# The per-layer embedding gate of a hybrid trunk: tokens as rows, and seven block products in place of eight

## The chip, the cores and the metric

The kernel runs on one core of one Trainium2 chip. The metric is the device time of one execution in microseconds (us). The engines are named as the profile names them: PE is TensorE's matmuls and PEld its weight loads, DVE is VectorE, ACT ScalarE, POOL GpSimd, SP SyncE, which here only issues transfers.

## The reference: what is computed

A trunk of four layers over 512 tokens of width 1024, in f32. Layer i uses a token mixer (gated linear attention GLA, latent attention MLA, a short convolution, and GLA again), then a squared-ReLU MLP of width 4096, then an embedding gate of its own:

```python
x = layer_norm(ALPHA * x + h, ln_g[i, 0], ln_b[i, 0])
x = layer_norm(ALPHA * x + sq_relu_mlp(x, mlp_w1[i], mlp_w2[i]), ln_g[i, 1], ln_b[i, 1])
x = x + jax.nn.sigmoid(x @ ple_w_gate[i]) * (p[i] @ ple_w_proj[i])
```

The change is in the third line: a 512x1024 by 1024x1024 product (the gate), and beside it a 512x256 by 256x1024 product (the projection).

## The kernel before, in words

**Matmuls.** Every f32 operand that matters is split into a high part (a cast to fp32r on ScalarE, line 87) and a low part (the difference, on VectorE, line 88). `mm3` (lines 113 to 117) then makes three matmuls of each product: high by high, high by low, low by high. Weights come by SyncE's queue into one of 4 buffers `raw` of 1 MB (`wget`, line 92) and are split in two pieces of 1024 columns (`wsplit`) into one of 4 buffers `wh`/`wl`. So at most four weights stand ready, and a split can't begin before an older weight has been used up. Activations and other large tiles share ten buffers named `r`, half-width ones eight named `t`; PSUM has eight banks, `ps`.

**Order.** TensorE runs in the order in which the program emits its instructions. For the other engines the framework draws up a fixed order when it builds the program; the kernel does not set it, apart from a few "issue after" edges. Work that TensorE is to do a little later is put into a list, `pend`, and run from it at set places (`flush`).

**MLP.** `up(g)` makes 512 columns of the hidden layer as a transposed activation, `down(g)` multiplies 1024 of them by their block of `mlp_w2` and adds the result into the residual tiles `xn[0..3]`, 128 tokens by 1024 each, tokens as rows. `down` already works by Winograd's form of Strassen's scheme: the 512x1024 by 1024x1024 product is cut into 2x2 blocks, and seven block products (`product`) do instead of eight, at the price of sums of activation blocks (lines 302, 305, 312, 315) and of weight blocks (`wadd`, line 108). Each product is 2 groups of 12 matmuls of 512 columns, and what it leaves in PSUM is added to `xn` on VectorE (lines 287, 289). The last one, `down(3)`, also normalises: `ln_half` takes the statistics of a half tile (line 151), `ln_apply` applies them (lines 155 to 159).

**The gate, `ple`.** It works with features as rows. First the projection, 8 groups of 6 matmuls, copied out by ScalarE (line 336); between these groups `ln_tr` transposes the four normalised tiles (line 165) and splits them, which gives the transposed x in high and low parts. Then 8 groups, one for each 128 output features, of 24 matmuls of 512 columns each (`stat_group`): for each, VectorE sums the two parts of x back (line 351), ScalarE takes the sigmoid (366), VectorE multiplies by the projection and adds x (367, 368). The result, still features as rows, is split for the next layer; and for the residual it is transposed back by TensorE (line 377, `back`, through `pend`), copied by ScalarE (380) and stored to DRAM in eight column blocks (381). In the last layer it goes to the output (370; the last block in two halves, lines 360 to 363), which the host turns.

**The next layer.** GLA starts with the first two heads' keys, MLA with a token-major latent product, the convolution with its `c` block. Each takes the transposed x as it is and flushes the remaining transposes of `pend` early on.

Of the kernel before, what the change touches and what calls it, by code (L numbers as in the profile page):

```python
# [18 lines left out]
P = 128  # L19
# [30 lines left out]
def trunk(ctx: ExitStack, tc: tile.TileContext, I: dict, out: bass.AP, layers=range(DEPTH)):  # L50
# [155 lines left out]

    def add_norm(lhs, unit, xn, gb, scaled, pre=None):
# [23 lines left out]
    def mlp(i, x, xn):  # L231
# [24 lines left out]

        def down(g, gb=None):
            h0, h1 = hid.pop(2 * g), hid.pop(2 * g + 1)  # L260
            lo, hi = slice(0, 256), slice(256, 512)
            a11, a21, a12, a22 = h0[:, :, lo], h0[:, :, hi], h1[:, :, lo], h1[:, :, hi]
            sts = [small(12, f"st{t}", 1) for t in range(NT)] if gb is not None else None
            banks = {}
            fresh = set()

            def weights(hf, c):
                return wget(I["mlp_w2"][i, hf, 2 * g + c])


            def product(a, w, name, th, hf, op):
                st = ring([P, 2, 4, 256], F32R)
                split(st[:, 0], st[:, 1], a)
                wh, wl = v3(wsplit(w), 512)
                for q in range(2):
                    first = (name, q) not in banks
                    if first:
                        banks[name, q] = bank()
                    ps = banks[name, q]
                    c = slice(q * P, q * P + P)  # L280
                    for k in range(4):
                        mm3(ps, (st[:, 0, k, c], st[:, 1, k, c]), (wh[:, k, :], wl[:, k, :]),
                            first and k == 0, k == 3, not first)
                    t = 2 * th + q
                    z = xn[t][:, hf * 512 : hf * 512 + 512]
                    if g == 0 and (t, hf) not in fresh:
                        V.scalar_tensor_tensor(out=z, in0=z, scalar=ALPHA, in1=ps, op0=ALU.mult, op1=op)
                    else:
                        V.tensor_tensor(out=z, in0=z, in1=ps, op=op)  # L289
                    fresh.add((t, hf))  # L290
                    if gb is not None and (th, hf, name) in ((0, 0, "d"), (0, 1, "b"), (1, 0, "c"), (1, 1, "b")):
                        if (t, hf) not in halves:
                            halves.add((t, hf))
                            ln_half(xn[t], sts[t], hf)
                            if (t, 1 - hf) in halves:
                                ln_apply(xn[t], sts[t], gb)

            halves = set()
            add, sub = ALU.add, ALU.subtract
            b11, b12, b22 = weights(0, 0), weights(1, 0), weights(1, 1)  # L300
            product(a11, b11, "b", 0, 0, add)
            V.tensor_tensor(out=a11, in0=a11, in1=a21, op=sub)
            wadd(b22, b12)
            product(a11, b22, "c", 1, 1, sub)
            V.scalar_tensor_tensor(out=a11, in0=a11, scalar=-1.0, in1=a22, op0=ALU.mult, op1=sub)
            wadd(b22, b11)
            product(a11, b22, "b", 1, 0, add)
            b21 = weights(0, 1)
            product(a12, b21, "d", 0, 0, add)
            wadd(b22, b21)  # L310
            product(a22, b22, "c", 1, 0, add)
            V.tensor_tensor(out=a21, in0=a22, in1=a21, op=sub)
            wadd(b12, b11)
            product(a21, b12, "b", 1, 1, sub)
            V.scalar_tensor_tensor(out=a11, in0=a11, scalar=-1.0, in1=a12, op0=ALU.mult, op1=sub)
            product(a11, weights(1, 1), "b", 0, 1, sub)
# [8 lines left out]
        return new_xT()  # L325

    def ple(i, x, xn, last):
        pT = v3(wload(I["pT"][i], 1024), 512)
        wp = v3(wload(I["ple_proj"][i]), 1024)
        proj = [ring([P, 4, T]) for _ in range(2)]  # L330
        for db in range(KB):
            ps = bank()
            for k in range(2):
                c = slice(db * P, db * P + P)
                mm3(ps, (wp[0][:, k, c], wp[1][:, k, c]), (pT[0][:, k, :], pT[1][:, k, :]), k == 0, k == 1)
            A.copy(proj[db // 4][:, db % 4, :], ps)
            if db in (0, 1, 5, 7):
                t = {0: 2, 1: 3, 5: 0, 7: 1}[db]
                ln_tr(t, xn[t], *x)
        if not last:  # L340
            nh, nl = new_xT()
            xd = dp.tile([T, D], F32, tag="xd", name=nm("xd"))
        else:
            nh = nl = xd = None
        ins = None
        for db in range(KB):
            if db % 2 == 0:
                wg = v3(wload(I["ple_gate"][i, db // 2]), 256)
            xh, xl = xk(x, db)
            xs = tmp()  # L350
            V.tensor_tensor(out=xs, in0=f(xh), in1=f(xl), op=ALU.add)
            sg = tmp()
            if last and db == KB - 1:
                ps = bank()
                for q in range(2):
                    sl = slice(256 * q, 256 * q + 256)
                    stat_group(wg, db % 2, x, sl=sl, o=ps)
                for q in range(2):
                    sl = slice(256 * q, 256 * q + 256)
                    A.activation(sg[:, sl], ps[:, sl], AF.Sigmoid)  # L360
                    V.tensor_tensor(out=sg[:, sl], in0=sg[:, sl], in1=proj[db // 4][:, db % 4, sl], op=ALU.mult)  # L361
                    V.tensor_tensor(out=sg[:, sl], in0=sg[:, sl], in1=xs[:, sl], op=ALU.add)  # L362
                    SP.dma_start(out[db * P : db * P + P, sl], sg[:, sl])
                continue
            ps = stat_group(wg, db % 2, x)
            A.activation(sg, ps, AF.Sigmoid)
            V.tensor_tensor(out=sg, in0=sg, in1=proj[db // 4][:, db % 4, :], op=ALU.mult)
            V.tensor_tensor(out=sg, in0=sg, in1=xs, op=ALU.add)
            if last:
                SP.dma_start(out[db * P : db * P + P, :], sg)  # L370
                continue
            ins = split(nh[db // 4][:, db % 4, :], nl[db // 4][:, db % 4, :], sg)

            def back(sg=sg, db=db):
                ps = bank().rearrange("p (t q) -> p t q", q=P)
                for t in range(NT):
                    PE.transpose(ps[:, t, :], sg[:, t * P : t * P + P], ident)
                o = tmp()
                o3 = o.rearrange("p (t q) -> p t q", q=P)
                A.copy(o3, ps)  # L380
                SP.dma_start(xd.rearrange("(t p) d -> p t d", p=P)[:, :, db * P : db * P + P], o3)

            pend.append(back)
            if len(pend) > 2:
                flush(1)
        return (nh, nl), xd, ins
# [11 lines left out]
    def gla(i, j, x, xd, first=None):  # L398
# [9 lines left out]
        for k in range(KB):  # L408
            for h in range(2):
                c = slice(h * P, h * P + P)  # L410
                mm3(pss[h], (w[0][:, k, c], w[1][:, k, c]), xk(x, k), k == 0, k == KB - 1)
# [303 lines left out]
    def mla(i, x, xd, dep):  # L715
# [19 lines left out]
        for t in range(NT):  # L735
            hk = {6: lambda t=t: c_tr(t - 1)} if t else {5: flush}
# [201 lines left out]
    def conv(i, x, xd):  # L938
        oT = []
        xn = None  # L940
        for u in range(4):
# [3 lines left out]
            ct, zt = [], []  # L945
            for cb in range(2):
                ps = stat_group(wc[0], cb, x)
                c = tmp()
                ci = A.copy(c, ps)
                ct.append(c)  # L950
                flush()
# [47 lines left out]
    for i in layers:  # L999
# [6 lines left out]
        x2 = mlp(i, xln, xn)  # L1006
        x, xd, dep = ple(i, x2, xn, i == layers[-1])
# [20 lines left out]
def _layout(a):  # L1028
# [38 lines left out]
    o["ple_gate"] = np.stack([_stat(w) for w in a["ple_w_gate"]])  # L1067
# [23 lines left out]
def build(nc, arrays, layers=range(DEPTH)):  # L1091
# [3 lines left out]
    out = nc.dram_tensor("out_0_dram", (D, T), F32, kind="ExternalOutput").ap()  # L1095
# [13 lines left out]
```

## Time and profile before

| | us |
|---|---|
| median of 3 runs | 2404.61 |
| lowest and highest | 2404.25, 2406.12 |
| the profiled execution's own time | 2405.31 |
| its span, first to last instruction | 2403.4 |
| mean granted TensorE clock | 0.998 |

The span is what the rows of the profile lie in; the time of an execution holds 1.9 us more. In a group's row stand line, engine, operation, output and inputs, shape, count, then busy time and mean length of one, then idle time of the engine ahead of it and what ended it. In a row of the timeline stand start, length, the same names, and in brackets the idle time ahead. In a row of busy times by stage, each engine's busy us and its number of instructions.

### The profile page before, as it was taken

How to read it: one execution, taken by the hardware profiler on the slowest of the kernel's cores; microseconds unless marked ns; L12 is line 12 of the kernel's file. 1: busy time of each engine (PE TensorE's matmuls, PEld its weight loads, DVE VectorE, ACT ScalarE, POOL GpSimd, SP SyncE). 2: the span in 40 equal slices, each digit the busy share in tenths (PEclk: the TensorE clock that was granted, in tenths of full speed). 3: DMA queues.
4: the chain of work that ended last, by engine and by line, in shares of the span. 5: the costliest groups of instructions: out<-in, count | busy, mean ns of one | idle time of the engine just before them, and what ended most of it. 6: DMA issues, size and time to landing. Idle time of an engine off the chain costs nothing. (4 is left out here: it accounts for less than half of the span.)

```text
span 2403.4 us, 28319 instructions
## 1 busy us (share of the span) xinstructions
PE 2375.0 (99%) x11394; PEld 1994.8 (83%) x11394; DVE 1692.8 (70%) x2092; ACT 1077.3 (45%) x1542; POOL 206.7 (9%) x200
## 2 busy tenths in 40 slices
PE   8999999999999999999999999999999999999998
PEld 7888888888888888888888888888887888888887
DVE  7777577689686666688744657768947766766885
ACT  6453445445464354444522244445454443544452
POOL 1541000000000000000000000000005510000000
PEclk9999999999999999999999999999999999999999
DMA  6222242234323222333434224323441222223430
GB/s 230 76 94 99 86 142 89 88 141 150 112 84 110 106 79 97 140 140 114 145 103 156 73 86 140 120 77 129 159 135 53 89 105 106 89 88 139 140 114 35
DMA packets 55346, 267.78 MB, mean 111 GB/s; under 512 B 5680, under 2 KB 18736, under 8 KB 27056
## 3 DMA queue, kind: packets, MB, share of 16 engines
q1 hardware_dynamic: 52272, 256.55, 30.5%
q10 hardware_dynamic: 2304, 8.39, 1.0%
q8 instruction: 89, 1.46, 0.2%
q0 software_dynamic: 640, 1.05, 0.2%
q14 instruction: 41, 0.34, 0.0%
HBM read 256.53 MB, written 8.39 MB: 110 GB/s over the span
## 5 line engine op out<-in xcount | busy, mean ns | idle before, releaser
L88 DVE TENSOR_TENSOR wl<-raw,wh 128x1024 fp32r<-128x1024 f32 x510 | 623.1, 1237 | 356.1 <-ACT wh L87 356.1
L87 ACT CAST wh<-raw 128x1024 fp32r<-128x1024 f32 x510 | 520.1, 1048 | 575.4 <-PE ps L116 262.9
L115 PE MATMUL ps<-r,wh 128*128 128x512 f32 (+1 forms) x1896 | 715.0, 377 | 4.0 <-ACT r L87 4.0
L116 PE MATMUL ps<-r,wh 128*128 128x512 f32 (+1 forms) x1896 | 710.8, 375 | 1.4 <-DVE r L88 0.9
L117 PE MATMUL ps<-r,wl 128*128 128x512 f32 (+1 forms) x1896 | 710.1, 375 | 0.0
L115 PE MATMUL ps<-wh,r 128*128 128x512 f32 x1328 | 520.1, 392 | 0.0
L117 PE MATMUL ps<-wh,r 128*128 128x512 f32 x1328 | 517.0, 389 | 0.0
L116 PE MATMUL ps<-wl,r 128*128 128x512 f32 x1328 | 516.8, 389 | 0.0
L115 PEld LDWEIGHTS ps<-r,wh 128*128 128x128 f32 x1896 | 357.8, 189 | 67.5 <-ACT r L87 5.0
L116 PEld LDWEIGHTS ps<-r,wh 128*128 128x128 f32 x1896 | 357.8, 189 | 66.5 <-DVE r L88 4.1
L117 PEld LDWEIGHTS ps<-r,wl 128*128 128x128 f32 x1896 | 357.5, 189 | 63.7
L117 PEld LDWEIGHTS ps<-wh,r 128*128 128x128 f32 x1328 | 249.3, 188 | 52.0
L115 PEld LDWEIGHTS ps<-wh,r 128*128 128x128 f32 x1328 | 249.4, 188 | 50.7
L116 PEld LDWEIGHTS ps<-wl,r 128*128 128x128 f32 x1328 | 249.5, 188 | 50.6
L147 POOL TENSOR_TENSOR rs<-rs,nhalf 128x1 f32<-128x1 f32 (+2 forms) x44 | 59.8, 1358 | 1826.5 <-DVE rs L146 1826.5
L87 ACT CAST r<-r 128x1024 fp32r<-128x1024 f32 x112 | 116.7, 1049 | 136.2 <-PE ps L117 80.1
L88 DVE TENSOR_TENSOR r<-r,r 128x1024 fp32r<-128x1024 f32 x112 | 136.4, 1221 | 42.4 <-ACT r L87 42.4
L289 DVE TENSOR_TENSOR xn<-xn,ps 128x512 f32<-128x512 f32 x192 | 130.7, 681 | 46.9 <-PE ps L117 46.9
L108 DVE TENSOR_TENSOR raw<-raw,raw 128x1024 f32<-128x1024 f32 x128 | 151.6, 1221 | 1.1
L234 ACT ACTIVATE t<-ps 128x512 f32<-128x512 f32 x128 | 76.1, 595 | 156.0 <-PE ps L117 156.0
L87 ACT CAST r<-ps 128x512 fp32r<-128x512 f32 x84 | 46.6, 591 | 95.1 <-PE ps L165 80.9
L480 ACT ACTIVATE t<-t 128x512 f32<-128x512 f32 (+2 forms) x64 | 37.4, 590 | 107.4 <-POOL t L544 74.9
(192 smaller groups left out, 1865.2 us busy)
## 6 DMA issues: line engine op xcount, KB each, us to landing
raw<-in_mlp_w SPq DMA_DIRECT2D x144, 1024.0 KB, 4.9
raw<-in_ple_gate SPq DMA_DIRECT2D x16, 1024.0 KB, 5.6
raw<-in_conv_in SPq DMA_DIRECT2D x12, 1024.0 KB, 5.0
raw<-in_gla_v SPq DMA_DIRECT2D x8, 1024.0 KB, 5.6
raw<-in_gla_r SPq DMA_DIRECT2D x8, 1024.0 KB, 4.9
raw<-in_gla_out SPq DMA_DIRECT2D x8, 1024.0 KB, 5.0
xd<-t SPq DMA_DIRECT2D x24, 256.0 KB, 3.7
xn<-xd ACTq DMA_DIRECT2D x12, 512.0 KB, 3.9
```

What stands on the lines that cost most here:

```text
L87: A.copy(h, src)
L88: return V.tensor_tensor(out=l, in0=src, in1=f(h), op=ALU.subtract)
L108: V.tensor_tensor(out=dst[:, s], in0=dst[:, s], in1=a[:, s], op=ALU.add)
L115: PE.matmul(o, ah, bh, start=start, stop=False, skip_group_check=more)
L116: PE.matmul(o, ah, bl, start=False, stop=False, skip_group_check=more)
L117: PE.matmul(o, al, bh, start=False, stop=stop, skip_group_check=more)
L147: G.tensor_tensor(out=dst, in0=dst, in1=nhalf[:, :n], op=ALU.pow)
L234: A.activation(r, ps, AF.Relu)
L289: V.tensor_tensor(out=z, in0=z, in1=ps, op=op)
L480: exps.append(A.activation(o, a, AF.Exp, scale=1.0 / TAU))
```

## The change

The seven products of `down` move into a function of their own, `seven(a, b, sink, order, before)`, where `a` and `b` are the four blocks of the activation and of the weight, `order` the order of the products and `sink` what is done with a finished group of 12 matmuls. `down` calls it with its old order, 1, 7, 6, 2, 4, 5, 3.

`ple` is written anew and calls it too. Tokens are now rows of the result. `raw_tr` transposes the normalised tiles without splitting them, `project` makes the projection token by token, and `seven` runs in the order 1, 2, 7, 6, 4, 5, 3, with the blocks so named that products 1 and 2 read tokens 256 to 511. `turn` transposes and splits the finished tiles for the next layer.

```diff
+        def raw_tr(t):
+            for c in range(2):
+                ps = bank().rearrange("p (k q) -> p k q", q=P)
+                for k in range(4):
+                    PE.transpose(ps[:, k, :], xn[t][:, (c * 4 + k) * P : (c * 4 + k + 1) * P], ident)
+                A.copy(xr[c][:, :, t * P : t * P + P], ps)
...
+        def finish(t, hf, src, sign, w):
+            a = acc.pop((t, hf), None) or tmp()
+            for c0 in range(hf * 512, hf * 512 + 512, w):
+                c = slice(c0, c0 + w)
+                b = slice(c0 - hf * 512, c0 - hf * 512 + w)
+                g = a[:, b]
+                A.activation(g, src[:, b], AF.Sigmoid, scale=sign)
+                V.tensor_tensor(out=g, in0=g, in1=proj[t // 2][:, t % 2, c], op=ALU.mult)
+                ins[0] = V.tensor_tensor(out=xn[t][:, c], in0=xn[t][:, c], in1=g, op=ALU.add)
+                if last:
+                    SP.dma_start(out[t * P : t * P + P, c], xn[t][:, c])
+            done.add((t, hf))
+            if not last and (t, 1 - hf) in done:
+                SP.dma_start(xd[t * P : t * P + P, :], xn[t])
+
+        def sink(th, q, hf, ps, op, first, final):
+            t = 2 * (1 - th) + q
+            sign = 1.0 if op == ALU.add else -1.0
+            if first and final:
+                finish(t, hf, ps, sign, 256 if last and q else 512)
+            elif first:
+                acc[t, hf] = tmp()
+                A.mul(acc[t, hf], ps, sign)
+            else:
+                g = acc[t, hf]
+                V.tensor_tensor(out=g, in0=g, in1=ps, op=op)
+                finish(t, hf, g, 1.0, 512)
+            if not last and th == 0 and hf == 1 and q == 0:
+                turn(0)
+
+        def turn(t):
+            if not nx:
+                nx.append(new_xT())
+            ln_tr(t, xn[t], *nx[0])
+
+        raw_tr(2)
+        project(0)
+        raw_tr(3)
+        project(1)
+        project(2)
+        raw_tr(0)
+        project(3)
+        seven((xr[0][:, :, hi], xr[0][:, :, lo], xr[1][:, :, hi], xr[1][:, :, lo]),
+              {f"{c + 1}{hf + 1}": I["ple_gate"][i, hf, c] for c in range(2) for hf in range(2)},
+              sink, (1, 2, 7, 6, 4, 5, 3), {2: [lambda: raw_tr(1)]})
+        if last:
+            return None, None, None
+        turn(1)
+        pend.extend(lambda t=t: turn(t) for t in (2, 3))
+        return nx[0], xd, ins[0]
```

The core of `seven`, in `down` as in `ple`:

```diff
+        plan = {
+            1: (lambda: (a11, get("11")), "b", 0, 0, add),
+            2: (lambda: (a12, get("21")), "d", 0, 0, add),
+            7: (s3, "c", 1, 1, sub),
+            6: (s2, "b", 1, 0, add),
+            4: (t4, "c", 1, 0, add),
+            5: (s1, "b", 1, 1, sub),
+            3: (s4, "b", 0, 1, sub),
+        }
+        for n, p in enumerate(order):
+            ready, name, th, hf, op = plan[p]
+            av, w = ready()
+            st = ring([P, 2, 4, 256], F32R)
+            split(st[:, 0], st[:, 1], av)
+            wh, wl = v3(wsplit(w), 512)
+            for fn in before.get(p, ()):
+                fn()
+            for q in range(2):
...
+                for k in range(4):
+                    mm3(ps, (st[:, 0, k, c], st[:, 1, k, c]), (wh[:, k, :], wl[:, k, :]),
+                        first and k == 0, k == 3, not first)
+                later = any(plan[m][2:4] == (th, hf) for m in order[n + 1 :])
+                sink(th, q, hf, ps, op, (th, hf) not in seen, not later)
```

The functions `s3`, `s2`, `t4`, `s1`, `s4` hold the sums: `s3`, `s2` and `s1` one activation sum and one weight sum each, `t4` a weight sum, `s4` an activation sum and a second fetch of block 22.

Two transposes of the finished tiles (of tiles 2 and 3) remain for the next layer and are run there from `pend`. MLA runs them at steps 2 and 6 of its first group; GLA (of layer 3) and the convolution make their first two groups in halves of 256 tokens, tokens 0 to 255 first, with a flush of one after each. The output is now stored with tokens as rows, and the host no longer turns it; `ple_gate` is laid out in blocks like `mlp_w2`.

More of the change, by code (lines that the diff above doesn't have):

```diff
@@ L203, in nat_group, with seven, get, s3 @@
         return ps
+    def seven(a, b, sink, order, before={}):
+        a11, a21, a12, a22 = a
+        banks, raw, seen = {}, {}, set()
+        add, sub = ALU.add, ALU.subtract
+        def get(n):
+            if n not in raw:
+                raw[n] = wget(b[n])
+            return raw[n]
+        def s3():
+            V.tensor_tensor(out=a11, in0=a11, in1=a21, op=sub)
+            get("12")
+            wadd(get("22"), raw["12"])
+            return a11, raw["22"]
+        def s2():
+            V.scalar_tensor_tensor(out=a11, in0=a11, scalar=-1.0, in1=a22, op0=ALU.mult, op1=sub)
+            wadd(raw["22"], raw["11"])
+            return a11, raw["22"]
+        def t4():
+            wadd(raw["22"], get("21"))
+            return a22, raw["22"]
+        def s1():
+            V.tensor_tensor(out=a21, in0=a22, in1=a21, op=sub)
+            wadd(raw["12"], raw["11"])
+            return a21, raw["12"]
+        def s4():
+            V.scalar_tensor_tensor(out=a11, in0=a11, scalar=-1.0, in1=a12, op0=ALU.mult, op1=sub)
+            return a11, wget(b["22"])
+        plan = {
[16 more added lines that the diff above has]
+            for q in range(2):
+                first = (name, q) not in banks
+                if first:
+                    banks[name, q] = bank()
+                ps = banks[name, q]
+                c = slice(q * P, q * P + P)
+                for k in range(4):
[3 more added lines that the diff above has]
+                sink(th, q, hf, ps, op, (th, hf) not in seen, not later)
+            seen.add((th, hf))
     def add_norm(lhs, unit, xn, gb, scaled, pre=None):
@@ L261, in down @@
             lo, hi = slice(0, 256), slice(256, 512)
-            a11, a21, a12, a22 = h0[:, :, lo], h0[:, :, hi], h1[:, :, lo], h1[:, :, hi]
             sts = [small(12, f"st{t}", 1) for t in range(NT)] if gb is not None else None
[L264 to L296, printed above, removed]
@@ L298, in down @@
-            halves = set()
[L299 to L316, printed above, removed]
+            halves = set()
+            def sink(th, q, hf, ps, op, first, last):
+                t = 2 * th + q
+                z = xn[t][:, hf * 512 : hf * 512 + 512]
+                if g == 0 and first:
+                    V.scalar_tensor_tensor(out=z, in0=z, scalar=ALPHA, in1=ps, op0=ALU.mult, op1=op)
+                else:
+                    V.tensor_tensor(out=z, in0=z, in1=ps, op=op)
+                if gb is not None and last:
+                    ln_half(xn[t], sts[t], hf)
+                    halves.add((t, hf))
+                    if (t, 1 - hf) in halves:
+                        ln_apply(xn[t], sts[t], gb)
@@ L318, in mlp @@
+            seven((h0[:, :, lo], h0[:, :, hi], h1[:, :, lo], h1[:, :, hi]),
+                  {f"{c + 1}{hf + 1}": I["mlp_w2"][i, hf, 2 * g + c] for c in range(2) for hf in range(2)},
+                  sink, (1, 7, 6, 2, 4, 5, 3))
         up(0)
@@ L324, in mlp, with ple @@
         down(3, load_gb(i, 1))
-        return new_xT()
-    def ple(i, x, xn, last):
+    def ple(i, xn, last):
+        lo, hi = slice(0, 256), slice(256, 512)
         pT = v3(wload(I["pT"][i], 1024), 512)
         wp = v3(wload(I["ple_proj"][i]), 1024)
[L330 to L353, printed above, removed]
-                ps = bank()
[L355 to L386, printed above, removed]
@@ new lines, in ple @@
+        xr = [ring([P, 4, T]) for _ in range(2)]
+        proj = [ring([P, 2, D]) for _ in range(2)]
+        acc = {}
+        xd = None if last else dp.tile([T, D], F32, tag="xd", name=nm("xd"))
+        def raw_tr(t):
[4 more added lines that the diff above has]
+                A.copy(xr[c][:, :, t * P : t * P + P], ps)
@@ L407, in gla @@
         pss = [bank(), bank()]
[L408 to L411, printed above, removed]
+        if first is None:
+            for half in range(2):
+                for h in range(2):
+                    stat_group(w, h, x, sl=slice(half * 256, half * 256 + 256), o=pss[h])
+                    flush(1)
+        else:
+            for k in range(KB):
+                for h in range(2):
+                    c = slice(h * P, h * P + P)
+                    mm3(pss[h], (w[0][:, k, c], w[1][:, k, c]), xk(x, k), k == 0, k == KB - 1)
         for h in range(2):
@@ L1005, in trunk @@
             xln, xn = conv(i, x, xd if xd is not None else I["x"])
-        x2 = mlp(i, xln, xn)
-        x, xd, dep = ple(i, x2, xn, i == layers[-1])
+        mlp(i, xln, xn)
+        x, xd, dep = ple(i, xn, i == layers[-1])
 def _stat(w, cols=256):
```

32 lines of the change are left out of this document (25 added, 7 removed).

## Prediction

> **What bounds the kernel now.** I read the page first, then the waits of TensorE, then the busy times by stage, and last the timelines of TensorE and VectorE around one embedding gate, that of layer 0.
>
> ```profile
> span 2403.4 us, 28319 instructions
> ...
> PE 2375.0 (99%) x11394; PEld 1994.8 (83%) x11394; DVE 1692.8 (70%) x2092; ACT 1077.3 (45%) x1542; POOL 206.7 (9%) x200
> ```
>
> TensorE (PE) is busy 99% of the span, so over the whole kernel each matmul taken away should count. Its own waits hold one entry that belongs to this change (columns: total, times, longest):
>
> ```profile
> PE ps L115 <- ACT r L87: 9.2, 5, 5.2
> ```
>
> One of the five, 5.2 us, is the kernel's start. The other four share 4.0 us: one per layer, at the first gate matmul. The averages hide a second thing, which the busy times by stage show (the gate's stage of layer 0 begins at 574.9; the last three rows are the 53 us around the same place in layers 1 to 3):
>
> ```profile
> core 0: us, PE busy (x) PEld busy (x) DVE busy (x) ACT busy (x) POOL busy (x), PEclk, DMA share, GB/s
> 536.50:574.90 38.40, 38.40 (x172) 31.73 (x171) 37.65 (x46) 18.88 (x21) 1.79 (x2) 1.00 0.43 151
> 574.90:589.50 14.60, 13.45 (x75) 11.07 (x73) 14.60 (x22) 9.87 (x18) 4.02 (x3) 1.00 0.02 3
> 599.70:641.00 41.30, 41.30 (x199) 34.27 (x198) 25.71 (x35) 18.44 (x28) 0.00 (x0) 1.00 0.42 136
> 1100.50:1153.50 53.00, 51.84 (x244) 42.78 (x243) 52.24 (x67) 28.73 (x38) 5.81 (x4) 1.00 0.32 111
> 1670.20:1723.20 53.00, 51.85 (x245) 42.79 (x243) 52.25 (x67) 28.75 (x38) 5.81 (x4) 1.00 0.32 110
> 2300.40:2353.40 53.00, 51.88 (x245) 42.84 (x243) 52.22 (x66) 28.75 (x38) 5.81 (x4) 1.00 0.32 110
> ```
>
> In the last down-projection of the MLP and the projection behind it VectorE (DVE) has no room: 37.65 of 38.40 us, then 14.60 of 14.60, and about 52.2 of 53 in each other layer. Only in the gate itself does it breathe, 25.71 of 41.30. The change puts more VectorE work exactly there. So the question is not the 70% but whether VectorE keeps its dates in a stage that it enters without a lead. ScalarE, at 9.87 of 14.60 and 18.44 of 41.30, has room for the casts that come with it.
>
> **TensorE, what goes.** The timeline of layer 0:
>
> ```profile
> 574.89 1.03 PE L165 MATMUL ps<-ident,xn 128*128 128x128 f32 x8
> 575.68 0.48 PE L115 MATMUL ps<-wh,wh 128*128 128x512 f32 x1
> ...
> 576.46 0.39 PE L115 MATMUL ps<-wh,wh 128*128 128x512 f32 x1
> ...
> 587.48 1.04 PE L165 MATMUL ps<-ident,xn 128*128 128x128 f32 x8
> 589.51 0.50 PE L115 MATMUL ps<-r,wh 128*128 128x512 f32 x1 [1.00 <-ACT r L87]
> 590.24 0.50 PE L116 MATMUL ps<-r,wh 128*128 128x512 f32 x1 [0.22 <-DVE r L88]
> ...
> 590.80 0.39 PE L115 MATMUL ps<-r,wh 128*128 128x512 f32 x1
> ...
> 606.22 0.39 PE L117 MATMUL ps<-r,wl 128*128 128x512 f32 x1
> ```
>
> A matmul's length (0.39) overlaps its neighbours, so the price is the distance of starts: from 590.80, the 4th gate matmul, to 606.22, the 72nd, 15.42 us / 68 = 0.2268 us. The gate has 8 x 8 x 3 = 192 matmuls a layer; seven products have 7 x 2 x 4 x 3 = 168. 24 fewer are 5.44 us a layer, 21.8 in all. The Trainium skill speaks against the change here: TensorE: Matmul & The Clock Gate, Back-to-back issue gap, gives 131 ns for a matmul of 512 columns in a stream of weight loads and matmuls, by which 96 matmuls are an estimated 12.6 us and the whole result would be 9.2 us worse. The trace disagrees with 0.2268, and the trace decides.
>
> The wait goes too. Eight transposes take 575.68 - 574.89 = 0.79 us and delay the matmuls behind them by another 0.10 (three starts in 0.78 instead of 0.68). Without a wait the 4th gate matmul would start at 587.48 + 0.79 + 0.78 = 589.05; it starts at 590.80, 1.75 late. After the change product 1 and product 2 read tokens 256 to 511 only, whose transposes lie well ahead, and token tile 1 is transposed behind product 1. So 1.75 x 4 = 7.0 us go. Transposes and projection stay in number: 32 ahead (now of raw values), 32 behind (now `turn` in place of `back`), 48 projection matmuls.
>
> Small change: matmuls split in two by columns. At the kernel's end stand 256-column ones:
>
> ```profile
> 2394.35 0.28 PE L115 MATMUL ps<-r,wh 128*128 128x256 f32 x1
> ...
> 2397.83 0.28 PE L117 MATMUL ps<-r,wl 128*128 128x256 f32 x1
> ```
>
> 29 steps in 3.48 us are 0.12 each, two for 0.24 against 0.2268. The last output block had 48 of them and loses them: 0.3 us gained. The starts of layers 2 and 3 (conv, GLA) take 96 each in place of 48 wide ones: 2 x (11.5 - 10.9) = 1.3 lost. The tail behind the last matmul, about 5.3 us to the span's end, keeps its form: sigmoid, product, sum and store on 256 columns.
>
> **VectorE, what comes.** The rows that price it:
>
> ```profile
> 551.14 1.22 DVE L88 TENSOR_TENSOR wl<-raw,wh 128x1024 fp32r<-128x1024 f32 x1
> 552.28 0.68 DVE L289 TENSOR_TENSOR xn<-xn,ps 128x512 f32<-128x512 f32 x1
> 552.88 1.22 DVE L88 TENSOR_TENSOR wl<-raw,wh 128x1024 fp32r<-128x1024 f32 x1
> ...
> 569.41 1.23 DVE L88 TENSOR_TENSOR wl<-raw,wh 128x1024 fp32r<-128x1024 f32 x1 [0.32 <-ACT wh L87]
> ...
> 581.15 0.64 DVE L88 TENSOR_TENSOR r<-ps,r 128x512 fp32r<-128x512 f32 x1
> 581.70 0.15 DVE L146 TENSOR_SCALAR rs<-mv 128x1 f32<-128x1 f32 x1
> ...
> 582.95 0.69 DVE L88 TENSOR_TENSOR r<-ps,r 128x512 fp32r<-128x512 f32 x1
> 583.55 1.28 DVE L159 SCALAR_TENSOR_TENSOR xn<-xn,rs,r 128x1024 f32<-128x1024 f32 x1
> 584.75 2.48 DVE L88 TENSOR_TENSOR r<-ps,r 128x512 fp32r<-128x512 f32 x4
> ...
> 591.30 4.63 DVE L88 TENSOR_TENSOR wl<-raw,wh 128x1024 fp32r<-128x1024 f32 x4
> 595.84 0.69 DVE L351 TENSOR_TENSOR t<-r,r 128x512 f32<-128x512 f32 x1
> ...
> 597.58 0.69 DVE L367 TENSOR_TENSOR t<-t,r 128x512 f32<-128x512 f32 x1
> 598.30 0.69 DVE L368 TENSOR_TENSOR t<-t,t 128x512 f32<-128x512 f32 x1
> ```
>
> Four pieces of 1024 columns advance VectorE by 595.84 - 591.30 = 4.54, 1.135 each; one of 512 columns by 583.55 - 582.95 = 0.60, or 0.72 (597.58 to 598.30) where the next needs its result. Per product there are 2 pieces to split the weight, 1 to split the activation, 2 for a weight sum (products 7, 6, 4, 5) and 1 for an activation sum (7, 6, 5, 3): in the order 1, 2, 7, 6, 4, 5, 3 that is 3, 3, 6, 6, 5, 6, 4, together 33 pieces against 8 now. A finished half tile costs add, product and sum, 0.60 + 0.72 + 0.60 = 1.92; products 2, 4 and 5 finish two each (3.84), product 3 two without the add (2.64), and `turn` has 8 splits. Half-width instructions fall from 40 to 30. Net growth is 25 x 1.135 - 10 x 0.60 = 22.4 us a layer.
>
> Now the dates, in us from 574.89. TensorE without a wait: projection 48 x 0.2268 = 10.9 and three sets of transposes at 0.9 bring product 1 to 13.6; with 5.44 a product and one more set behind product 1, product 2 starts at 19.9, then 7, 6, 4, 5, 3 at 25.4, 30.8, 36.3, 41.7, 47.1; product 3 with `turn(0)` inside it ends at 53.5. VectorE: the normalisation of the last token tile ends at 584.75; without the two splits of transposes inside it (0.55 + 0.60), which become copies of ScalarE, at 583.6, that is 8.7. One weight piece of product 1 is done by then (the one at 569.41), 32 remain. I take the instructions in the order of emission, each as soon as it can run, since the rows of 551.14 to 552.88 show a finished sum of the MLP (L289) put between two halves of a weight split. Ready times: product 1 at 8.7 + 2 x 1.135 = 11.0; 2 at 14.4; 7 at 21.2; 6, behind product 2's finish, at 31.9 (date 30.8); 4 at 37.5; 5, behind product 4's finish, between 44.4 and 48.2 (41.7); 3 at 8.7 + 32 x 1.135 + 2 x 3.84 = 52.7 (47.1). So product 3 starts 5.6 us late in each layer: 22.4 in all. The bounds: if all finishing fell behind the preparing, VectorE would be through at 45.0 and product 3 on time, but `turn(0)` inside it needs 5.8 of that finishing and waits 1.0; if product 5's finish comes first as well, 3.84 more.
>
> Then the next layer. Conv and GLA start with tokens 0 to 255, whose last transposes stand directly ahead: the wait of 1.75 comes back twice, 3.5. MLA starts with tile 0 alone, but needs two new weights: to the second one TensorE has 5.44 + 3 x 0.9 + 12 x 0.2268 = 10.9 us from product 3's start, VectorE has 3.84 + 2.64 of finishing, 6 x 0.60 of `turn` and 3 pieces, 13.5; of the 2.6 between I count 2.0.
>
> Transfers I cost at nothing:
>
> ```profile
> raw<-in_ple_gate SPq DMA_DIRECT2D x16, 1024.0 KB, 5.6
> ...
> xd<-t SPq DMA_DIRECT2D x24, 256.0 KB, 3.7
> ```
>
> One gate block is fetched twice. Its second fetch waits on SyncE's queue for a raw buffer that product 4's weight sum frees, before 37; landing in 5.6 it is there by 43, and product 3's preparing begins only behind that of product 5, at 44 or later. The cover is about 1 us; if the queue holds it back, each us shows at product 3, and the next layer's weights stand behind it. The 8 stores a layer become 4 of twice the size.
>
> Sum, against the profiled execution's 2405.3 (2403.4 of span and 1.9 around it): -21.8 - 7.0 - 0.3 + 22.4 + 3.5 + 2.0 + 1.3 = +0.1. That execution lies 0.7 above the median of 2404.6, so I forecast 2405: no change.
>
> **Rivals.** *A, finishing slips behind preparing.* Then `turn(0)` waits 1.0 and the rest, some 3 us a layer, is met at the next layer's start, where three layers have one: 4 x 1.0 + 3 x 3 = 13 in place of 24.4. With the rest of the sum this gives about 2393; against it stands the prompt finish seen in the MLP, for it that VectorE would be 100% fed either way. *B, VectorE hides it all.* -21.8 - 7.0 - 0.3 + 3.5 + 1.3 = -24.3, about 2380. For it: 70% busy against 99%, and TensorE never waits in the MLP's own seven products; against it the windows, since there an up-projection ahead of each gives VectorE a lead. In the Trainium skill this is Perfetto Trace Analysis, Identifying the Most-Contended Engine: the engine of highest occupancy is the one to relieve. The rows by stage disagree for this stage. *C, slower: VectorE idles between the steps of a product.* Each activation goes sum on VectorE, cast on ScalarE, difference on VectorE, and VectorE's waits have
>
> ```profile
> DVE r L88 <- ACT r L87: 74.8, 69, 5.4
> ```
>
> 74.8 / 69 = 1.08 us a time. It decides as soon as VectorE has no other piece ready meanwhile. Unfilled in products 7, 6, 4, 5 and 3 it is 5.4 a layer, 21.6 in all, 2427; in half of them 2416.
>
> **Numbers.** About 0.2% (4.8 us) is what a measurement of this kernel can tell from no change. The even case has 0.42, by its bounds (1.0 below to 3.84 above per layer in part) from 2397 to 2412: 0.25 within 0.2%, 0.09 below, 0.08 above. A has 0.30, B 0.06, C 0.22. Faster 0.45, same 0.25, slower 0.30. The range 2386 to 2417 leaves out B, the low end of A and the high end of C.
>
> **What would show it.** Right: VectorE near 1780 us busy; in each gate VectorE without idle time from the normalisation on; TensorE waits of about 1 us ahead of product 6 and of 2 to 5 ahead of 5, ended by VectorE, and little ahead of 4 and 3; the old wait of 1.0 gone from product 1 and found again at conv and GLA. Wrong: no TensorE wait inside the gate (B), finishing instructions behind product 3's splits (A), or VectorE idle for ScalarE while TensorE waits (C).

## The result, and the profile after

The changed kernel takes 2422.22 us (median of 4 runs, 2419.63 to 2424.58) against 2404.93 for the kernel before (4 runs, 2404.25 to 2406.12): a ratio of 1.0073, with an interval of 1.0060 to 1.0086. It is slower by 17.3 us. The forecast was 2405.0 with a range of 2386 to 2417, so the result lies outside it, on the side that had a chance of 0.30.

The head of the page of the changed kernel, from an execution of 2424.58 us:

```profile
span 2422.6 us, 28301 instructions
...
PE 2372.0 (98%) x11370; PEld 1987.8 (82%) x11370; DVE 1778.2 (73%) x2152; ACT 1126.9 (47%) x1594; POOL 208.4 (9%) x200
```

TensorE has 24 instructions fewer: 96 matmuls of the gate are gone, 96 wide ones at two layer starts have become 192 narrow ones, and the last 48 narrow ones have become 24 wide ones. Yet it is busy only 3.0 us less, and the span is 19.2 us longer. VectorE has grown by 85 us, to the 1780 that was forecast. TensorE's waits (total, times, longest) say where it stands:

```profile
PE ps L116 <- DVE wl L88: 16.5, 9, 2.3
PE ps L117 <- DVE r L88: 8.3, 4, 2.1
...
PE ps L116 <- DVE r L88: 1.7, 4, 0.5
```

The first two rows are the gates, three waits a layer: ahead of products 6 and 5 for the low half of the weight (one more of 0.3 stands inside a product 3), ahead of product 3 for the low half of the activation. VectorE makes all of them. The old wait at the first gate matmul is gone, and the third row is the starts of the convolution and of GLA.

The timeline of TensorE at product 6 in layer 0 shows a second thing, which the waits do not:

```profile
606.12 0.39 PE L115 MATMUL ps<-wh,r 128*128 128x512 f32 x1
608.51 0.50 PE L116 MATMUL ps<-wl,r 128*128 128x512 f32 x1 [2.00 <-DVE wl L88]
608.85 0.40 PE L117 MATMUL ps<-wh,r 128*128 128x512 f32 x1
609.08 0.59 PE L115 MATMUL ps<-wh,r 128*128 128x512 f32 x1
609.47 0.63 PE L116 MATMUL ps<-wl,r 128*128 128x512 f32 x1
```

After a wait of 2.00 us the same matmul takes 0.63 in place of 0.39, and the next starts come 0.43 apart in place of 0.227. The busy times by stage tell why. These stretches are 3.41 us each, laid so that one of them begins where the clock falls; the last row is the gate as a whole (busy us of PE, PEld, DVE, ACT, POOL, then the granted clock, DMA share and GB/s):

```profile
605.69:609.10 3.41, 1.41 (x7) 0.86 (x6) 3.41 (x4) 1.23 (x2) 0.00 (x0) 1.00 0.00 0
609.10:612.51 3.41, 3.41 (x10) 2.63 (x9) 3.41 (x4) 1.04 (x1) 0.00 (x0) 0.50 0.00 0
612.51:615.92 3.41, 3.41 (x16) 2.80 (x15) 3.05 (x4) 2.72 (x4) 0.00 (x0) 1.00 0.82 283
619.34:622.75 3.41, 1.97 (x9) 1.31 (x7) 3.12 (x5) 3.21 (x5) 0.00 (x0) 1.00 0.92 368
622.75:626.16 3.41, 2.48 (x9) 1.72 (x10) 3.41 (x5) 3.41 (x4) 0.00 (x0) 1.00 0.03 14
629.59:633.00 3.41, 1.34 (x6) 0.82 (x5) 3.41 (x5) 1.58 (x2) 0.00 (x0) 1.00 0.38 154
633.00:636.41 3.41, 3.39 (x10) 2.09 (x9) 3.41 (x4) 0.08 (x1) 0.00 (x0) 0.50 0.47 65
...
575.00:635.00 60.00, 53.49 (x235) 42.30 (x235) 58.28 (x68) 40.20 (x53) 5.49 (x3) 0.95 0.21 73
```

Twice TensorE stands for 2.0 us of a stretch (1.41 and 1.34 busy), and twice the whole next stretch is granted half the clock: 10 matmuls in 3.41 us where 16 stand in the stretch behind it. The four gates hold eight such stretches, and the distances of the starts in them add up to 12.1 us beyond the usual ones. Meanwhile VectorE is busy 58.28 of 60.00 us: it has nothing to spare, and hardly a gap.

### The profile page after: what moved, and what is told of

Same layout as the page of the kernel before. It is cut to its first block, busy times and chain, and to the rows that moved or that the text cites. A ratio compares the mean times of both kernels' runs of the same rounds, so it can differ in the third digit from the quotient of the medians.

```text
span 2422.6 us, 28301 instructions
## 1 busy us (share of the span) xinstructions
PE 2372.0 (98%) x11370; PEld 1987.8 (82%) x11370; DVE 1778.2 (73%) x2152; ACT 1126.9 (47%) x1594; POOL 208.4 (9%) x200
## 5 line engine op out<-in xcount | busy, mean ns | idle before, releaser
L116 PE MATMUL ps<-wl,r 128*128 128x512 f32 x1552 | 611.6, 394 | 16.6 <-DVE wl L88 16.5
L115 PE MATMUL ps<-r,wh 128*128 128x512 f32 (+1 forms) x1664 | 617.4, 371 | 1.1 <-ACT r L87 1.1
L117 PE MATMUL ps<-wh,r 128*128 128x512 f32 x1552 | 610.3, 393 | 8.3 <-DVE r L88 8.3
L116 PE MATMUL ps<-r,wh 128*128 128x512 f32 (+1 forms) x1664 | 614.8, 369 | 2.2 <-DVE r L88 1.7
L117 PE MATMUL ps<-r,wl 128*128 128x512 f32 (+1 forms) x1664 | 614.0, 369 | 0.0
L115 PE MATMUL ps<-wh,r 128*128 128x512 f32 x1552 | 613.4, 395 | 0.0
L116 PEld LDWEIGHTS ps<-wl,r 128*128 128x128 f32 x1552 | 294.7, 190 | 83.9 <-DVE wl L88 24.1
L116 PEld LDWEIGHTS ps<-r,wh 128*128 128x128 f32 x1664 | 314.1, 189 | 56.3 <-DVE r L88 4.2
L115 PEld LDWEIGHTS ps<-r,wh 128*128 128x128 f32 x1664 | 314.1, 189 | 54.0 <-ACT r L87 2.0
L117 PEld LDWEIGHTS ps<-r,wl 128*128 128x128 f32 x1664 | 313.9, 189 | 52.5
L117 PEld LDWEIGHTS ps<-wh,r 128*128 128x128 f32 x1552 | 294.7, 190 | 71.1 <-DVE r L88 9.9
L115 PEld LDWEIGHTS ps<-wh,r 128*128 128x128 f32 x1552 | 294.4, 190 | 60.2
L88 DVE TENSOR_TENSOR r<-r,r 128x1024 fp32r<-128x1024 f32 x140 | 170.2, 1221 | 42.6 <-ACT r L87 42.5
L108 DVE TENSOR_TENSOR raw<-raw,raw 128x1024 f32<-128x1024 f32 x160 | 189.6, 1220 | 1.1
```

Source lines behind the costliest of these rows:

```text
L88: return V.tensor_tensor(out=l, in0=src, in1=f(h), op=ALU.subtract)
L108: V.tensor_tensor(out=dst[:, s], in0=dst[:, s], in1=a[:, s], op=ALU.add)
L115: PE.matmul(o, ah, bh, start=start, stop=False, skip_group_check=more)
L116: PE.matmul(o, ah, bl, start=False, stop=False, skip_group_check=more)
L117: PE.matmul(o, al, bh, start=False, stop=stop, skip_group_check=more)
```

## The experiments

The main theory after the result: (1) VectorE is the bound of the gate, and sets its dates by the number of its pieces; (2) the waits that this gives TensorE also cost it the clock. Rivals: the new layout itself (tokens as rows, `turn`, the stores) costs the time; the finishing of half tiles stands in the wrong place; VectorE idles for ScalarE's casts (C of the prediction). All times stand beside runs of the kernel before on the same chip, whose median was 2404.65 to 2404.81 each time.

### Is it VectorE's work: the weight sums left out, all or half

```diff
-    def wadd(dst, a):
-        for c in range(0, 2048, PIECE):
+    def wadd(dst, a, pieces=2):
+        for c in range(0, pieces * PIECE, PIECE):
```

The gate calls it with 0 (`e3_no_sums`) or 1 (`e4_half_sums`) in place of 2, so it leaves out all the weight sums or the second half of each; everything else stays.

> The change with the eight pieces of weight sums of each gate left out (the gate's values are then not the reference's); everything else, TensorE's order included, as it is. It takes 8 x 1.135 = 9.1 us from VectorE per layer, more than the 7 us of waits. Theory: all waits in the gate and all of its half clock go: 2422 - 28 - 13.6 = about 2380. Rival (the waits come from the hops between VectorE and ScalarE, not from the amount of work): 2400 or more, with VectorE idle before them.

> As the run without weight sums, but only the second of the two pieces of each sum is left out: 4.5 us of VectorE per layer (the gate's values are again not the reference's). Theory: 2.5 us of waiting remain per layer, in waits too short for most of the half clock: 2422 - 18 - 7 to 13.6 = 2390 to 2397. Rival (no cost of the clock): 2404.

Without the sums the kernel takes 2391.25 us (2390.66 to 2392.59; ratio 0.9947, 0.9932 to 0.9962), with half of them 2396.71 (2396.05 to 2399.16; 0.9970, 0.9958 to 0.9982). Here is a waits row of each, first without sums, then with half of them:

```profile
PE ps L117 <- DVE r L88: 5.6, 4, 1.7
```

```profile
PE ps L116 <- DVE wl L88: 10.2, 5, 2.7
```

VectorE's 36.3 us of sums (32 pieces at 1.135) cost 31.0 us of the whole kernel's time. The first half of what is left out brings 25.5, the second only 5.5: by then the three waits a layer have shrunk to one, in layer 2 to two short ones (without sums it is at product 6, for the activation's own chain), and TensorE is nearly the bound again. So the saving of matmuls was there, and with the sums free the change would have been faster than before by 13.5. My expectation of 2380 for no sums was 11 too low. That chain, 5.6 us in all, is half of it. The waits and the half clock that I took off, 28 and 13.6, come to 26.4 and 12.1 in the account below, which is another 3.1; the rest stays open.

In the same 60 us as above, the run without sums has this row:

```profile
575.00:635.00 60.00, 58.34 (x281) 47.93 (x280) 59.35 (x70) 45.13 (x63) 4.36 (x3) 1.00 0.40 139
```

VectorE is as busy as before, 59.35 us, though 9.1 us of its work in the gate are gone: it must already be at later work, and TensorE hardly waits for it. So a full VectorE alone does not tell the bound; the waits of TensorE do.

### Is it the layout: tokens as rows, but eight plain block products

```diff
-        seven((xr[0][:, :, hi], xr[0][:, :, lo], xr[1][:, :, hi], xr[1][:, :, lo]), ...
+        for hf in range(2):
+            ws = [v3(wload(I["ple_gate"][i, hf, c]), 512) for c in range(2)]
+            for t in (2, 3, 0, 1) if hf == 0 else (0, 1, 2, 3):
...
+                ps = nat_group(lambda k, t: xk((xh, xl), k, slice(t * P, t * P + P)), ws, t)
+                finish(t, hf, ps, 1.0, ...)
...
```

Here the transposes are split as before the change, and 192 matmuls a layer are back.

> The gate with tokens as rows, but as 16 plain groups of 24 matmuls (eight block products): no sums, four weights split once, finished halves as in the change. Theory: VectorE's work is back near that of before, so no wait inside the gate and full clock; the old wait of 1.75 a layer gone (7.0), 0.3 gained, 1.3 and 3.5 paid at conv and GLA: about 2402. Rival (it is the layout, its order and its hand-over to the next layer that cost): 2410 or more.

The kernel takes 2405.46 us (10 runs, 2403.99 to 2406.66; ratio 1.0004, 0.9994 to 1.0013), the same as before. So the new layout as a whole costs nothing, but it does not win the 2 to 3 us that I expected either: the old wait ahead of the gate is gone, and other waits take its place. The starts of convolution and GLA cost 2.3 us each (distances of starts beyond the usual), and each projection has a wait of its own, 0.7 us with what it delays:

```profile
PE ps L115 <- DVE rs L146: 2.2, 4, 0.5
```

The seven products are thus worth +16.8 us (2422.22 - 2405.46), of which their matmuls are -21.8; what they bring along costs 38.6.

### How much of it is the clock: TensorE kept at work in the waits

```diff
+        def idle(n):
+            ps = bank().rearrange("p (k q) -> p k q", q=P)
+            for _ in range(n):
+                PE.matmul(ps, ones, ones.unsqueeze(1).broadcast_to([P, NT, P]), start=True, stop=True)
...
-              sink, (1, 2, 7, 6, 4, 5, 3), {2: [lambda: raw_tr(1)]})
+              sink, (1, 2, 7, 6, 4, 5, 3), {2: [lambda: raw_tr(1)]}, {p: [lambda: idle(8)] for p in (6, 5, 3)})
```

Eight matmuls whose result nobody reads stand ahead of products 6, 5 and 3.

> Ahead of products 6, 5 and 3 of the gate, where TensorE waits 2.0 to 2.4 us, eight matmuls of 512 columns on constants are put into TensorE's order; their result is read by nobody. Theory (the waits cost 7 us a layer, and each can be followed by 3.41 us at half clock, eight times in the profile, about 1.7 us each): VectorE's dates do not move, so nothing is won or lost in the waits themselves, but TensorE is no longer idle and the half clock goes: 2422 - 13 = about 2409, granted clock back at 0.997. Rival (the half clock falls into time that TensorE would wait anyway, and the loss is the waits alone): 2420 to 2424.

The kernel takes 2415.12 us (2414.77 to 2415.45; ratio 1.0045, 1.0030 to 1.0060): with 96 matmuls more it is 7.1 us faster than the changed one. The timeline at product 6:

```profile
605.08 1.98 PE L426 MATMUL ps<-ones 128*128 128x512 f32 x8
606.89 0.39 PE L115 MATMUL ps<-wh,r 128*128 128x512 f32 x1
607.14 0.50 PE L116 MATMUL ps<-wl,r 128*128 128x512 f32 x1
607.48 0.40 PE L117 MATMUL ps<-wh,r 128*128 128x512 f32 x1
607.72 0.39 PE L115 MATMUL ps<-wh,r 128*128 128x512 f32 x1
```

The filling ends as the low half of the weight comes, and the rows behind it keep 0.39. No gate of this run has a stretch at half clock; its mean clock is 0.998, as before the change (0.992 after it). What is left of the delay is VectorE's alone: 24 idle matmuls of 0.227 and 1.56 us of waits (2.0 in layer 1), about 7.0 us a layer. I had expected 2409, some 13 us back. Part of the half clock is no loss of its own, since TensorE would have waited for VectorE a little later anyway: VectorE's lateness is 28.5 us in the four gates here, idle matmuls and waits together, against 26.4 in the changed kernel. The runs differ by 7.1, the profiled executions by 9.6.

### What makes the clock fall: waits put into a kernel that has none

The base is `e7_eight_handover` (below), which has neither waits of 2 us nor half clock in its gates. Three times a gate, TensorE is made to wait for a chain of copies on ScalarE:

```diff
+        def hold():
+            ps = bank()
+            PE.matmul(ps[:, :P], ones, ones, start=True, stop=True)
+            j, h = tmp(), tmp(F32R)
+            A.copy(j[:, :P], ps[:, :P])
+            for _ in range(HOPS):
+                A.copy(j[:, :P], j[:, :P])
+            A.copy(h[:, :P], j[:, :P])
+            PE.matmul(ps[:, :P], ones, h[:, :P], start=True, stop=True)
...
+                if (hf, t) in ((0, 0), (1, 0), (1, 2)):
+                    hold()
```

HOPS is 4 in `e11_holds`, 0 in `e12_short_holds`.

> The eight products with the early hand-over (2401 us, VectorE with room to spare), and three waits put into each gate: a small matmul, six short copies of ScalarE one behind the other, and a small matmul that needs the last of them. By the rows for such copies (0.3 to 0.37 us) TensorE should wait about 2 us each time, as in the change, 12 times. Theory (waits of about 2 us are followed by 3.41 us at half clock about two times in three, and where VectorE has room nothing takes that back): the waits, some 26 us, and 8 x 1.7 us on top, about 2440. Rival (the half clock in the change came from VectorE's load or from the products themselves): the waits alone, 2427, clock 0.998.

> The same with two copies in place of six, so waits of about 1 us. Theory (the half clock needs a wait of about 2 us; those of 1.0 to 1.8 us in the runs so far had none): the waits alone, 12 us, 2413, clock 0.998. Rival (any wait can bring it): 2413 plus several times 1.7.

The times are 2452.41 us (2451.55 to 2459.09; ratio 1.0207, 1.0190 to 1.0224) and 2426.67 (2425.77 to 2428.10; 1.0091, 1.0076 to 1.0106). Both are some 12 to 14 us above my expectation, first because the holds came out longer than planned: 12 waits of 33.8 us in the one, nine of 2.43 and three of 3.75 to 4.06, and of 15.9 us in the other, nine of 1.11 and three of 1.93 to 2.04 (in the first three layers ScalarE has other work ahead of the middle one). Each hold also costs 0.5 to 0.7 beside its wait, which I hadn't counted. The rest is the clock: behind the long holds stand six stretches at half clock, 9.1 us of the 51.1 over the base; behind the short ones two, 3.0 of 25.4, and both of these stand behind waits of about 2 us, none behind the nine of 1.11.

The two holds of 1.93 us are the telling pair. Stretches of the run with short holds, the hold of layer 0 and the stretch behind it, then those of layer 1:

```profile
611.75:615.16 3.41, 1.75 (x9) 1.26 (x7) 3.28 (x4) 2.69 (x6) 0.00 (x0) 1.00 0.00 0
615.16:618.57 3.41, 3.14 (x14) 2.63 (x15) 2.65 (x3) 1.17 (x3) 0.00 (x0) 1.00 0.52 159
...
1181.78:1185.19 3.41, 1.48 (x8) 1.12 (x7) 3.38 (x5) 2.84 (x5) 0.00 (x0) 1.00 0.38 94
1185.19:1188.60 3.41, 3.41 (x10) 2.63 (x9) 1.09 (x1) 0.00 (x0) 0.00 (x0) 0.50 0.87 303
```

The waits are equally long. The first is cut in two by the border at 615.16, 1.66 us before it and the rest behind, and the clock stays; the second lies wholly in one stretch, 1.93 us, and the next stretch is halved. That explains the changed kernel too: its wait of 2.29 us ahead of product 5 in layer 0 is split (1.97 and 2.48 busy, above), and it is the only one of the three there without a stretch at half clock.

### Could GpSimd take the sums

The sums of products 7 and 5 go to GpSimd, in pieces of 512 columns; in `e8_pool_behind` with an "issue after" edge behind its last step of the normalisation, in `e5_pool_sums` without.

```diff
-            V.tensor_tensor(out=dst[:, s], in0=dst[:, s], in1=a[:, s], op=ALU.add)
+            if side:
+                with tc.issue_after(rstds[-1].ins):
+                    side.tensor_tensor(out=dst[:, s], in0=dst[:, s], in1=a[:, s], op=ALU.add)
...
```

> The change with the weight sums of products 7 and 5 of each gate on GpSimd, in pieces of 512 columns; the output is the reference's. It takes the same 4.5 us a layer from VectorE as the run with half of the sums. Theory: if GpSimd does not hinder VectorE, the time is that of the half sums, 2396 to 2400. Rival (both slow each other down, as the rows of before suggest where a 512-column sum takes GpSimd 1.98 us and VectorE's neighbour 0.90 in place of 0.69): 2405 or more.

> The weight sums of products 7 and 5 on GpSimd again, but issued behind GpSimd's last step of the normalisation, ahead of which they stood in the run before. Theory (what cost there was the wait of 4.7 us a layer for the normalisation, not the sums themselves): that wait goes, and the time is that of the half sums, 2396 to 2400. Rival (GpSimd's sums and VectorE hinder each other): 2410 or more.

Neither helps: they take 2428.72 us (ratio 1.0096, 1.0079 to 1.0113) and 2429.89 (1.0105, 1.0091 to 1.0119). Without the edge the sums stood ahead of the normalisation's own GpSimd step, and TensorE waited 4.5 us a layer for the normalised tile. With it the wait only moved, to 5.2 us a layer at product 7. GpSimd's rows and then VectorE's of that stretch:

```profile
584.14 17.52 POOL L111 TENSOR_TENSOR raw<-raw,raw 128x512 f32<-128x512 f32 x8
```

```profile
587.06 4.54 DVE L88 TENSOR_TENSOR r<-r,r 128x1024 fp32r<-128x1024 f32 x2
591.52 6.77 DVE L88 TENSOR_TENSOR wl<-raw,wh 128x1024 fp32r<-128x1024 f32 x3
598.22 4.53 DVE L113 TENSOR_TENSOR raw<-raw,raw 128x1024 f32<-128x1024 f32 x2
602.67 1.21 DVE L88 TENSOR_TENSOR wl<-raw,wh 128x1024 fp32r<-128x1024 f32 x1
```

While GpSimd adds, each of VectorE's pieces takes 2.26 us in place of 1.135; the first one after GpSimd's last is back at its old price. In those 17.5 us GpSimd does the work of four pieces, and VectorE loses about eight. `e10_pool_more`, which also gives the second pieces of the sums of products 6 and 4 to GpSimd (and has the hand-over of the last part below), shows it larger still: it takes 2442.39 us (1.0159, 1.0145 to 1.0173), with 10.8 us of wait at product 7.

> As the run with hand-over, and the second piece of the sums of products 6 and 4 on GpSimd too: 2.3 us of VectorE less per layer, but GpSimd's 2.9 us for a piece then stand in the chain of a product. Theory: VectorE is the bound still, so 1 to 2 us a layer are gained: about 2390. Rival (the chain through GpSimd is longer than the two pieces on VectorE): 2395 to 2405.

### Does the order of VectorE's work matter: finishing behind preparing

In layers 0 to 2 the finishing of product 4 is held back until product 3's operands are ready and that of product 2 behind `turn(1)`, and `turn(0)` stands behind product 3. This makes rival A of the prediction, but for product 5's finishing, which stays where it was.

```diff
-            if not last and th == 0 and hf == 1 and q == 0:
-                turn(0)
...
+                if hf == 0 and not last:
+                    held[t] = ready
+                else:
+                    ready()
...
+              sink, (1, 2, 7, 6, 4, 5, 3), {2: [...], 3: [lambda: held.pop(0)(), lambda: held.pop(1)()] if not last else []})
...
+        turn(0)
         turn(1)
+        held.pop(2)()
+        held.pop(3)()
```

> The change with the finishing of products 2 and 4 emitted behind the preparing of product 3 (layers 0 to 2; layer 3 as it is), and the transposes of tile 0 behind product 3: case A of the prediction. Theory (VectorE's order decides where the wait falls): waits ahead of products 6, 5 and 3 nearly gone in layers 0 to 2, 2 to 4 us instead at the hand-over to the next layer, little half clock there: about 2404. Rival (the same work only waits elsewhere): 2418 to 2424.

The kernel takes 2419.54 us (2418.87 to 2419.83; ratio 1.0061, 1.0046 to 1.0076), 2.7 below the changed kernel. In the three layers so changed the gate's waits are gone, and the same time stands behind product 3:

```profile
PE ps L116 <- DVE wl L88: 8.9, 3, 4.9
...
PE ps L117 <- DVE wl L88: 6.3, 3, 3.1
...
PE ps L165 <- DVE xn L394: 4.4, 3, 2.1
```

Behind layer 0 TensorE waits 2.23 us for the finished tile and 5.46 for MLA's weights (distances of starts beyond the usual), and behind layers 1 and 2 it has several waits of 0.8 to 3.4, with up to three stretches of half clock in a row. The order of VectorE's work moves the waits and hardly the time.

### What is worth keeping: the hand-over

The finished tile 2 is turned directly behind tile 1, not from `pend`, so that only tile 3 stands ahead of the next layer's second half.

```diff
-        pend.extend(lambda t=t: turn(t) for t in (2, 3))
+        turn(2)
+        pend.append(lambda: turn(3))
```

> Eight products with tokens as rows, and tile 2 transposed directly behind tile 1, so that at conv and GLA its 0.8 us cover a part of the wait for tile 1 and tile 3 is transposed one group ahead of its use. Theory: of the 2.2 us of waits at each of these two starts 1.8 go: 3.6 in all, 2402. Rival (the waits follow ScalarE's and VectorE's queues, not the order of transposes): 2405.

> The same with tile 2 transposed directly behind tile 1, as in the eight products with that hand-over, where it won 4 us. Theory: the same 2 us at conv and at GLA again, some 4 us below the run beside it, 2393 to 2396, and so faster than both kernels. Rival (product 3's finishing comes later here than with eight products, so tile 2 is not ready behind tile 1, and TensorE waits there instead): no gain.

With the eight plain products of `e2_eight_rows` this gives 2401.29 us (10 runs, 2400.94 to 2402.89; ratio 0.9987, 0.9978 to 0.9997): 3.5 us faster than the kernel before and 20.9 faster than the changed one, the fastest of the kernels that leave nothing out. The 2.3 us at each of the starts of convolution and GLA are down to 0.4. The gate's stretch has room on VectorE (38.91 of 60.00 us) and TensorE works through:

```profile
575.00:635.00 60.00, 59.46 (x282) 49.19 (x283) 38.91 (x51) 25.50 (x37) 4.36 (x3) 1.00 0.35 123
```

The same edit on the kernel with GpSimd's sums (`e9_behind_handover`) gives 2425.78 (1.0089, 1.0075 to 1.0102), 4.1 below `e8_pool_behind`. On the changed kernel alone it wasn't tried; by these two it would give back about 4 of the 17.3.

## Why the prediction was wrong

The sum of the prediction, term by term, beside what the profiled execution has (distances of starts beyond the usual, all four layers):

| term | forecast | measured |
|---|---|---|
| 96 matmuls | -21.8 | -21.8 |
| old wait at product 1 | -7.0 | -6.7 |
| VectorE's lateness in the gate | +22.4 | +26.4 |
| starts of convolution and GLA | +3.5 | +5.0 |
| start of MLA | +2.0 | +0.4 |
| narrow matmuls, both ways | +1.0 | taken as +1.0 |
| half clock in the gate | not in the sum | +12.1 |
| gaps under 0.4 us each, from the gate on for 110 us | not in the sum | +2.7 |
| sum | +0.1 | +19.1 |

The spans differ by 19.2. A longer stretch of half clock in GLA of layer 0 is another 1.4, and a shorter one in GLA of layer 3 takes 1.1 back; the change touches neither, and the account closes to a few tenths of a us.

**Right.** The saving of TensorE is real: without the sums the kernel falls 13.5 below the one before. VectorE as the bound of the gate, its instruction prices and its total (1780 forecast, 1778.2 measured) held, as did the wait that goes. Rival B is excluded by the three waits in each gate. So is A: the changed kernel's VectorE finishes before it prepares (the rows below), and `e6_late_finish`, which puts A in place but for product 5's finishing, ends at 2419.5, not 2393; A priced the waits behind product 3 too low, and the clock not at all. The second fetch of a block cost nothing, as forecast: product 3 waits for its activation (2.07 us for `r`), not for a weight.

**C gave nearly the time, but not by its mechanism.** Its upper value was 2427, by VectorE idling for ScalarE's casts. VectorE idles 1.7 of 60 us in the gate. The time fits by chance.

**Wrong: the zero of VectorE's dates.** The step "the dates, in us from 574.89" let TensorE and VectorE start together at the first transposes. But six projection matmuls stood ahead of them, which the timeline of the kernel before shows:

```profile
573.29 0.39 PE L117 MATMUL ps<-wh,r 128*128 128x512 f32 x1
573.52 0.39 PE L115 MATMUL ps<-wh,wh 128*128 128x512 f32 x1
...
574.65 0.39 PE L117 MATMUL ps<-wh,wl 128*128 128x512 f32 x1
```

The last product of the MLP ends at 573.52, and 6 x 0.227 = 1.4 us of the 10.9 that I counted as projection were over at 574.89. VectorE's 8.7 is 10.1 from the stage's true start, and product 3 is late by 5.6 + 1.4 = 7.0 us a layer. That is what `e1_filled` has at full clock. Four layers make 5.6 us more, and this alone would have moved the forecast from 2405.0 to 2410.6.

**Wrong: the places.** I had about 1 us ahead of product 6, 2 to 5 ahead of 5 and little ahead of 3. Measured are 2.16, 2.45 and 2.23 in layer 0, so only the one ahead of 5 is where it was forecast. VectorE takes its work in the order that I assumed, product 2's finish before product 6's weight:

```profile
601.95 0.68 DVE L411 TENSOR_TENSOR t<-t,ps 128x512 f32<-128x512 f32 x1
602.54 0.69 DVE L393 TENSOR_TENSOR t<-t,r 128x512 f32<-128x512 f32 x1
...
606.63 0.69 DVE L394 TENSOR_TENSOR xn<-xn,t 128x512 f32<-128x512 f32 x1
607.23 2.35 DVE L88 TENSOR_TENSOR wl<-raw,wh 128x1024 fp32r<-128x1024 f32 x2
...
618.40 0.69 DVE L411 TENSOR_TENSOR t<-t,ps 128x512 f32<-128x512 f32 x1 [0.42 <-PE ps L117]
...
621.12 0.69 DVE L411 TENSOR_TENSOR t<-t,ps 128x512 f32<-128x512 f32 x1 [0.29 <-PE ps L117]
```

The last two rows show the way back: at half clock TensorE finishes a product later, and VectorE, the bound, now waits for it (0.42, 0.29). That the loop of the two engines hands on part of the clock's loss is argued from these rows, not tried by itself.

**Wrong: no term for the clock.** The prediction read PEclk as 1.00 in every stage that it looked at and never asked what waits of 2 us do to it. The kernel before could have told: its granted clock is halved in GLA of layers 0 and 3. In layer 0, TensorE stands for 1.99 us of one stretch and the next is halved:

```profile
50.17:53.58 3.41, 1.42 (x11) 0.98 (x9) 2.44 (x3) 0.49 (x1) 3.41 (x1) 1.00 0.45 132
53.58:56.99 3.41, 3.20 (x12) 2.92 (x13) 2.20 (x4) 1.35 (x2) 0.72 (x2) 0.50 0.43 180
```

`e1_filled` prices the clock at 7.1 us between the medians. The run at full clock also has some 3 us more than the kernel before of gaps under 0.4 us each, which I hadn't counted. With 5.6 for the zero and 0.3 for the old wait that makes about 16 of the 17.3 us; the starts of the next layers, 1.5 above the forecast at convolution and GLA and 1.6 below it at MLA, cancel.

## What to carry to other kernels

When a change moves work to an engine with room on average, date that engine's pieces from the moment the stage really begins, and count the lead that it enters with; in a stage entered without any, each piece over the bound shows in full. A TensorE wait of about 2 us costs more than its length, since the clock may be halved for 3.41 us behind it, and matmuls that do nothing can pay. What counts is the idle time within one stretch of 3.41 us: two waits of 1 us are cheaper than one of 2 only where they lie in different ones. And try before giving sums of two inputs to GpSimd: here VectorE lost more by it than it was spared.

## What the runs showed of the hardware

**The clock goes by a fixed grid.** Within each of the fourteen profiled executions all changes of the granted clock lie whole multiples of 3.4133 us apart (the falls of the changed kernel at 609.10, 633.00, 1189.37 and 1199.61 are 7, 163 and 3 of them apart). I laid that grid over them all, from 25 us on, and took for each stretch the time in which no matmul ran. With 1.95 us or more of it the next stretch was at half clock, 81 times of 81. Below that, where the stretch itself was at full clock, it was so 6 times of 17 with 1.66 to 1.94, and never in 75 with 1.0 to 1.65. The idle time may be in parts: `e6_late_finish` has a stretch with waits of 1.14, 0.89 and 0.62 us, and the next one is halved. A stretch that is at half clock already needs less: it was followed by another one 41 times of 41 with 0.57 us or more without a matmul, and 0 times of 66 with 0.52 or less. This is how the rows of two and three halved stretches come about. A halved stretch costs about 1.5 us of matmuls (12.1 us for eight). The Trainium skill, TensorE: Matmul & The Clock Gate, What's actually happening, states a free-running window of 3413 ns, with which the runs agree, and gives an idle window as what halves the clock; here a window idle for 57% is enough. The phase differs from run to run, and by it whether a wait is split. This may be why the changed kernel's runs spread over 5 us and the kernel before's over 2: the fastest of the four, 2419.63 us, has the highest mean clock, 0.995, and the slowest, 2424.58, the lowest, 0.992.

**VectorE at half speed beside GpSimd.** With two inputs from SBUF on both engines, VectorE's pieces take 2.26 us in place of 1.135 as long as GpSimd adds. The Trainium skill, SBUF — State Buffer, Who interferes with whom, says that such a pair contends for a shared read interface, with which the trace agrees. The measured factor of two is what turns the gift into a loss.
